# A transformer block on one core: a plain second MLP product, a coarser convolution and coarser modulation sums

## The chip, the cores and the metric

The kernel runs on one core of a Trainium2 chip. The metric is the device time of one execution, in microseconds (us). The core has a matrix engine (PE, whose weight loads the profile shows apart as PEld), a vector engine (DVE), a scalar engine (ACT), a general engine (POOL), and a queue for loads and stores (SP). Every engine works through its own list of instructions in order, and an instruction at the head of a list that waits for another engine holds up everything behind it on that list.

## The reference

One block of depth 1 works on 1024 tokens of width 1024, with 256 context tokens, all in fp32. Cut to what the change touches:

```python
mx = jnp.split((s_c @ w_ada[l] + b_ada[l])[:, None, :], N_ADA, axis=-1)      # six modulation vectors
qkv = jax.nn.silu(depthwise_conv_centred(concat([p[3], p[4], p[5]]), conv_w)) # 7 taps, 3 x 8 heads x 128
q = l2_normalize(hd(q)) * DN_HEAD_DIM ** -0.5
k = l2_normalize(hd(k))                                                       # x * rsqrt(sum(x*x) + eps)
h_x = layer_norm(ALPHA * h_x + mx[2] * y_x, ln1_g[l], ln1_b[l])
h_x = layer_norm(ALPHA * h_x + mx[5] * (jnp.square(jax.nn.relu(u @ w1)) @ w2), ln2_g[l], ln2_b[l])
```

`u @ w1` is 1024 x 1024 by 1024 x 4096, and the second MLP product is 1024 x 4096 by 4096 x 1024. The gated delta rule (DeltaNet) runs for 8 heads in both directions over chunks of 128 tokens. Then come 8 heads of differential attention over the same tokens.

## The kernel before, in words

Every large product is made of three matmuls of rounded parts: an operand is cast to fp32r by ACT (the high part), DVE or POOL subtracts that from the fp32 value (the low part), and hi x hi, hi x lo and lo x hi are added up in one PSUM bank. A matmul has a 128 x 128 left operand and a moving operand of up to 512 columns.

A scheduler inside the tile framework sets each engine's order from priorities and its own estimates of durations. `rank` puts a piece of work into one of several classes: the delta rule's chain and the weights come first (class 0), `dn_prep` and the inverse after them (1), the convolution after that (2).

The stages that the change touches, in order of time:

- **DeltaNet** (`dn_phase`, about 190 to 1330 us). Per head, `dn_proj` multiplies the tokens by a weight block for k, q and v, ACT copies the products into `cvraw`, and a convolution of 7 taps follows: one ACT row for the middle tap and six DVE rows `L441` for the others, for each stretch of `CW` = 256 columns. k and v have five such stretches (one of context, four of tokens), q has four. `dn_prep` builds chunk matrices; `rsqrt` (L126 to L137) takes the reciprocal root of the squared norms by a bit trick and four Newton rounds of three DVE rows (L134 to L136). `inverse32` (L547 to L578) inverts the diagonal blocks in one long chain of dependent DVE rows, `dn_double` completes the inverse on PE, and `dn_chain` walks the ten chunks in both directions (PE, DVE `xs` L674 and `S` L689, ACT). Its end calls `rsqrt` again, scales the head's output (L715), and PE transposes that (L719). POOL subtracts the low parts of the weights (L152).
- **Attention** (`da_all`, about 1330 to 2095 us). While a head's scores run, `ada_cols` adds up the modulation vectors of 4 or 5 column blocks of 128: per block four loads of 128 KB (`adraw`, two buffers, two rows of 128 columns per partition each) and eight DVE rows (L1461, L1463).
- **First MLP product** (`mlp_up`, to 2684 us): a Strassen-Winograd scheme with seven products in place of eight. It stays as it is.
- **Second MLP product** (`mlp_down`, from 2686 us to the end): the same scheme. The 32 row blocks of w2 are taken in six groups, the tokens in four pairs of blocks, and each group and pair has seven products. Per product DVE adds a bank of 512 columns into `acc` (L1421). Before that the sums and differences of the blocks must be made: of `araw` on DVE (L1329), of `braw` on POOL (L1325) after POOL has scaled it (L1365), and all seven forms of each are split (ACT L1320, DVE or POOL L1322). `feed` sets how far ahead the operands are made (`DAA`, `DBA`), and most operand tiles have one buffer. After its last product a token block gets its layer norm on DVE and is stored.

Of the kernel before, what the change touches and what calls it, by code (L numbers as in the profile page):

```python
# [17 lines left out]
P = 128  # L18
# [18 lines left out]
CW = 256  # L37
# [6 lines left out]
DAA, DBA = (14, 14)  # L44
LPB = (2, 3)
S1 = 8
AB = (2, 1, 1, 1, 1, 1, 1)
DG = (2, 2, 3, 3, 3, 3)
# [7 lines left out]
class K:  # L56
# [69 lines left out]
    def rsqrt(self, pool, x, n, tag):  # L126
# [6 lines left out]
        for _ in range(4):  # L133
# [283 lines left out]
    def dn_proj(self, h, nm, res):  # L417
# [6 lines left out]
        raw = self.dw.tile([P, T + 12], F32, name="cvraw", bufs=2)  # L424
        XO = CTX + 9
        nc.gpsimd.memset(raw[:, XO - 3:XO], 0.0)  # L426
        nc.gpsimd.memset(raw[:, XO + SEQ:XO + SEQ + 3], 0.0)
        if not isq:
            nc.gpsimd.memset(raw[:, 0:3], 0.0)
            nc.gpsimd.memset(raw[:, 3 + CTX:6 + CTX], 0.0)  # L430
            nc.gpsimd.dma_start(out=raw[:, 3:3 + CTX], in_=self.kvc_d[0 if nm == "k" else 1, h])
        self.gemm_cols(w, (self.uh, self.ul), TOKS_X, lambda ps, t0, n: nc.scalar.copy(out=raw[:, XO + t0:XO + t0 + n], in_=ps))
        acc = self.dw.tile([P, SEQ if isq else T], F32, name=nm + "T", bufs=BK[" vqk".index(nm)])
# [10 lines left out]
        res[nm] = acc  # L444

# [25 lines left out]
    def dn_prep(self, h, r):  # L471
# [7 lines left out]
        for c0, n in groups:  # L479
            pt = self.pt.tile([P, 4, P], F32, name="pt")  # L480
            for c in range(n):
                nc.tensor.transpose(out=pt[:, c, :], in_=ch(kT, c0 + c), identity=self.ident)
# [29 lines left out]
        for c0, n in ((0, NC0), (NC0, 4), (NC0 + 4, 4)):  # L512
            dec = [self.dn_decay(d, h, c0, n, c0 > 0) for d in range(2)]
            pk = self.pt.tile([P, 4, P], F32, name="pt")
            for c in range(n):
                nc.tensor.matmul(pk[:, c], lhsT=ch(kT, c0 + c), rhs=ch(kT, c0 + c), start=True, stop=True)
# [4 lines left out]
            if c0:  # L521
                pk = self.pt.tile([P, 4, P], F32, name="pt")
                for c in range(n):
                    nc.tensor.matmul(pk[:, c], lhsT=ch(kT, c0 + c), rhs=ch(qT, c0 + c - NC0), start=True, stop=True)
# [107 lines left out]
    def dn_pre(self, h, r):  # L632
# [13 lines left out]
        for c0, n in ((0, 4), (4, 4), (8, 2)):  # L646
            pt = self.pt.tile([P, 4, P], F32, name="pt")
            for c in range(n):
                nc.tensor.transpose(out=pt[:, c, :], in_=ch(kT, c0 + c), identity=self.ident)
# [3 lines left out]
    def dn_chain(self, h, r):  # L653
# [9 lines left out]
        for step in range(NT):  # L663
            for d in range(2):
# [6 lines left out]
                else:  # L671
                    nc.tensor.matmul(pc[:, 0], lhsT=ch(kT, c), rhs=S0, start=True, stop=True)
# [628 lines left out]
    def mlp_down(self):  # L1301
        nc, i = self.nc, self.i
        sizes = DG
        at = [sum(sizes[:g]) for g in range(len(sizes))]
# [343 lines left out]
```

## Time and profile before

| | |
|---|---|
| time, median of 3 runs | 3126.78 us (3111.26 to 3156.79) |
| profiled execution, time | 3127.75 us |
| its span, first to last instruction | 3126.0 us |
| PE busy | 2800.6 us, 90% |
| PE's weight loads busy | 2234.6 us, 71% |
| DVE busy | 2315.2 us, 74% |
| ACT busy | 1412.6 us, 45% |
| POOL busy | 984.9 us, 32% |
| mean granted PE clock | 0.951 of full |

The profile is one execution. Matmuls are pipelined, so that their busy time is longer than the distance from one to the next. A view by stages gives, for each stretch, its start and end, its length, the busy time of PE, PEld, DVE, ACT and POOL with the number of instructions in brackets, the share of full clock that PE was granted, the busy share of the DMA engines and the GB/s they moved. A row of waits names an instruction, what released it, the total in us, how often, and the longest. A timeline row has start, duration, engine, line, operation, output and inputs, and in square brackets the idle time before it and its releaser. A group of instructions has its count, the total busy us and the mean in ns, and the idle time before them.

### The profile page before, as it was taken

The page shows a single profiled execution, that of the slowest core. Times are in us where ns is not written, and L with a number is a line of the kernel's source. Part 1 is how long each engine was busy: PE and PEld are TensorE (multiplying, and loading weights), DVE is VectorE, ACT ScalarE, POOL GpSimd, SP SyncE. Part 2 cuts the span into 40 slices and gives each one's busy share as a digit, 9 for nine tenths or more (in the row PEclk, how much of TensorE's full clock was granted, in tenths as well). Part 3 has the DMA queues.
Part 4 walks back from the last instruction along what each step waited for, and adds up shares of the span by engine and source line. Part 5 has one row for each costly group of instructions (what it writes and reads, how often), then busy time and mean ns, then how long its engine had stood idle before and what let it go on. Part 6 is the DMA issues. An engine that isn't in the chain of part 4 may idle for free.

```text
span 3126.0 us, 46024 instructions
## 1 busy us (share of the span) xinstructions
PE 2800.6 (90%) x15736; PEld 2234.6 (71%) x15736; DVE 2315.2 (74%) x4654; ACT 1412.6 (45%) x3547; POOL 984.9 (32%) x973
## 2 busy tenths in 40 slices
PE   7988889899898989989999998999998999777887
PEld 4876668677686767768777776777776777566666
DVE  4658688886876856368888886646658775799989
ACT  4644335345453443335555555655546223233332
POOL 1245313423434242111111110001006433867770
PEclk9999979989998998999999998999999999898999
DMA  7521211211212122363333333127555443422222
GB/s 259 188 91 40 52 50 42 58 46 44 68 40 56 43 50 64 89 152 91 93 94 81 89 87 94 56 75 221 169 156 182 144 128 111 166 72 81 81 81 93
DMA packets 370043, 303.20 MB, mean 97 GB/s; under 512 B 89300, under 2 KB 321876, under 8 KB 368784
## 3 DMA queue, kind: packets, MB, share of 16 engines
q1 hardware_dynamic: 347920, 252.14, 27.5%
q10 hardware_dynamic: 18304, 37.41, 4.8%
q0 software_dynamic: 3584, 10.71, 0.9%
q8 instruction: 124, 2.03, 0.3%
q14 instruction: 111, 0.91, 0.1%
HBM read 212.08 MB, written 66.06 MB: 89 GB/s over the span
## 4 chain that ended last, share of the span: by engine, by line
PE 36%; DVE 16%; DMA 6%; issue 2%; ACT 2%; POOL 0%; SPq 0%; ACTq 0%; DVEq 0%; POOLq 0%
PE pat L912 4%; PE pg L970 4%; PE pg L972 4%; PE pg L971 4%; DVE A L1322 3%; PE pat L909 2%; PE pg L166 2%; PE pg L167 2%; PE pg L168 2%; PE pa L970 2%; DVE acc L1421 2%; PE pa L972 2%; PE pa L971 2%; PE sx L873 2%; PE sx L874 2%
## 5 line engine op out<-in xcount | busy, mean ns | idle before, releaser
L152 POOL TENSOR_TENSOR wlo<-wraw,whi 128x256 fp32r<-128x256 f32 x312 | 357.3, 1150 | 1224.3 <-ACT whi L151 891.4
L168 PE MATMUL pg<-uh,wlo 128*128 128x512 f32 x1152 | 483.4, 420 | 33.0 <-POOL wlo L152 32.8
L166 PE MATMUL pg<-uh,whi 128*128 128x512 f32 x1152 | 484.8, 421 | 12.6 <-ACT whi L151 6.5
L167 PE MATMUL pg<-ul,whi 128*128 128x512 f32 x1152 | 479.8, 416 | 0.0
L151 ACT CAST whi<-wraw 128x256 fp32r<-128x256 f32 (+1 forms) x568 | 240.9, 430 | 334.9 <-DMA wraw<-in_w_in_dram 98.5
L168 PEld LDWEIGHTS pg<-uh,wlo 128*128 128x128 f32 x1152 | 226.3, 196 | 80.4 <-POOL wlo L152 40.3
L166 PEld LDWEIGHTS pg<-uh,whi 128*128 128x128 f32 x1152 | 225.7, 196 | 53.6 <-ACT whi L151 7.8
L167 PEld LDWEIGHTS pg<-ul,whi 128*128 128x128 f32 x1152 | 225.3, 196 | 39.5
L152 DVE TENSOR_TENSOR wlo<-wraw,whi 128x256 fp32r<-128x256 f32 (+1 forms) x256 | 134.3, 533 | 117.8 <-ACT whi L151 113.6
L884 DVE TENSOR_REDUCE mp<-sx 128x1 f32<-128x1024 f32 x128 | 155.8, 1219 | 40.5 <-PE sx L874 40.1
L970 PE MATMUL pa<-B,A 128*128 128x512 f32 x256 | 109.7, 429 | 79.6 <-DVE acc L1421 45.3
L1320 ACT CAST A<-araw 128x384 fp32r<-128x384 f32 (+1 forms) x144 | 66.2, 476 | 238.7 <-DVE araw L1329 105.3
L889 ACT ACTIVATE p<-sx,mx 128x1024 f32<-128x1024 f32 x128 | 143.2, 1119 | 55.8 <-DVE mx L885 50.8
L912 PEld LDWEIGHTS pat<-V,aT 128*128 128x128 f32 x1280 | 149.2, 192 | 14.9 <-ACT aT L910 12.8
L912 PE MATMUL pat<-V,aT 128*128 128x128 f32 x1280 | 157.3, 278 | 0.0
L441 DVE SCALAR_TENSOR_TENSOR vT<-cvraw,taps,vT 128x256 f32<-128x256 f32 x240 | 120.4, 525 | 13.5 <-ACT vT L439 12.6
L1322 DVE TENSOR_TENSOR A<-araw,A 128x384 fp32r<-128x384 f32 (+1 forms) x144 | 126.6, 886 | 2.7 <-ACT A L1320 2.3
L909 PE MATMUL pat<-ident,p 128*128 128x128 f32 x640 | 119.3, 285 | 6.7 <-ACT aT L910 2.4
L970 PEld LDWEIGHTS pa<-B,A 128*128 128x128 f32 x256 | 51.7, 202 | 101.3 <-ACT A L1320 44.0
L1463 DVE SCALAR_TENSOR_TENSOR adacc<-adraw,s_cols,adacc 128x128 f32<-128x128 f32 x224 | 84.9, 379 | 52.1 <-DMA adraw<-in_w_ada_dram 48.3
L441 DVE SCALAR_TENSOR_TENSOR kT<-cvraw,taps,kT 128x256 f32<-128x256 f32 x240 | 114.9, 509 | 4.8 <-POOL cvraw L426 4.7
L909 PEld LDWEIGHTS pat<-ident,p 128*128 128x128 f32 x640 | 74.7, 142 | 56.7 <-ACT aT L910 22.6
(479 smaller groups left out, 7739.9 us busy)
## 6 DMA issues: line engine op xcount, KB each, us to landing
wraw<-in_w_in_dram SPq DMA_DIRECT2D x288, 128.0 KB
wraw<-in_w_in_dram SPq DMA_DIRECT2D x64, 256.0 KB
adraw<-in_w_ada_dram SPq DMA_DIRECT2D x128, 128.0 KB
uraw<-in_w_mlp_dram SPq DMA_DIRECT2D x32, 512.0 KB
braw<-in_w_mlp_dram SPq DMA_DIRECT2D x32, 512.0 KB
ff_d<-ue SPq DMA_DIRECT2D x52, 256.0 KB
araw<-ff_d SPq DMA_DIRECT2D x32, 384.0 KB
wa<-in_w_ada_dram SPq DMA_DIRECT2D x8, 1024.0 KB
```

The source lines that it names most:

```text
L151: nc.scalar.copy(out=hi, in_=raw)
L152: self.weng.tensor_tensor(out=lo, in0=raw, in1=hi.bitcast(F32), op=ALU.subtract)
L166: nc.tensor.matmul(o, lhsT=hi, rhs=a, start=k == 0, stop=False)
L167: nc.tensor.matmul(o, lhsT=hi, rhs=b, start=False, stop=False)
L168: nc.tensor.matmul(o, lhsT=lo, rhs=a, start=False, stop=k == KT - 1)
L441: nc.vector.scalar_tensor_tensor(out=a, in0=raw[:, t0 - 3 + j:t0 - 3 + j + n], scalar=self.taps[:, j, s:s + 1], in1=a, op0=ALU.mult, op1=A ...
L909: nc.tensor.transpose(out=pt[:, c], in_=a[:, (c0 + c) * P:(c0 + c + 1) * P], identity=self.ident)
L912: nc.tensor.matmul(po, lhsT=aT[:, c], rhs=r["v"][:, c], start=c == 0, stop=c == NT - 1)
L970: nc.tensor.matmul(ps, lhsT=ah, rhs=bh, start=k == 0 and not add, stop=False, **more)
L971: nc.tensor.matmul(ps, lhsT=ah, rhs=bl, start=False, stop=False, **more)
L972: nc.tensor.matmul(ps, lhsT=al, rhs=bh, start=False, stop=k == n - 1, **more)
L1322: eng.tensor_tensor(out=z[1], in0=x, in1=z[0].bitcast(F32), op=ALU.subtract)
```

## The change

- The second MLP product is a plain one: four groups of eight row blocks of w2, eight token blocks, 1024 output columns in two banks. That is 4 x 8 x 8 x 2 x 3 = 1536 matmuls of 512 columns, where 6 groups' seven products made 7 x 4 x 16 x 3 = 1344. Each row block of w2 is scaled (DVE) and split once (ACT cast, DVE subtraction), with 12 buffers for the split blocks, 3 for the raw ones; each token block of `ff` is split once per group, with 3 buffers. POOL does nothing there. `acc` is added to 64 times in place of 168.
- The convolution has two parts per tensor in place of five or four: the context and the tokens stand in one buffer with a gap of 8 columns, cut where the first product of 512 tokens ends. k and v have parts of 772 and 516 columns, q of 508 and 516; six DVE rows each, so 12 in place of 30 or 24. `ck` steps over the gap.
- `rsqrt` has three Newton rounds.
- `ada_cols` loads one row block of w_ada for all of a head's columns at once (320 or 256 KB, 640 or 512 columns per partition) into a single buffer and adds it in one DVE row: 8 loads and 8 rows per head in place of 16 or 20 loads and 32 or 40 rows.

```diff
@@ rsqrt
-        for _ in range(4):
+        for _ in range(3):
@@ dn_proj
-        raw = self.dw.tile([P, T + 12], F32, name="cvraw", bufs=2)
-        XO = CTX + 9
+        raw = self.dw.tile([P, T + GAP + 6], F32, name="cvraw", bufs=2)
+        XO = CTX + GAP + 3
...
-            c0 = 0 if isq else CTX
-            for t0, o, n in ([] if isq else [(3, 0, CTX)]) + [(XO + t, c0 + t, CW) for t in range(0, SEQ, CW)]:
-                a = acc[:, o:o + n]
-                nc.scalar.activation(out=a, in_=raw[:, t0:t0 + n], func=AF.Copy, scale=self.taps[:, 3, s:s + 1])
+            at = XO - 3 if isq else 0
+            cut = SPLIT if isq else CTX + GAP + SPLIT
+            for o, e in ((0, cut), (cut, acc.shape[1])):
+                a = acc[:, o:e]
+                nc.scalar.activation(out=a, in_=raw[:, at + 3 + o:at + 3 + e], func=AF.Copy, scale=self.taps[:, 3, s:s + 1])
                 for j in (0, 1, 2, 4, 5, 6):
-                    nc.vector.scalar_tensor_tensor(out=a, in0=raw[:, t0 - 3 + j:t0 - 3 + j + n],
+                    nc.vector.scalar_tensor_tensor(out=a, in0=raw[:, at + j + o:at + j + e],
                                                    scalar=self.taps[:, j, s:s + 1], in1=a, op0=ALU.mult, op1=ALU.add)
@@ mlp_down (the old body, shown above, is taken out)
+        G, NK = 4, 8
+        shapes = {"acc": ([P, NX, D], F32, 1), "mx5": ([P, D], F32, 1), "lng": ([P, D], F32, 2), "araw": ([P, NK, P], F32, 2),
+                  "braw": ([P, D], F32, 3), "A": ([P, 2, NK, P], F32R, 3), "B0": ([P, 2, D], F32R, 2), "B": ([P, 2, D], F32R, NB2 - 2)}
...
+        def split(z, x):
+            nc.scalar.copy(out=z[:, 0], in_=x)
+            nc.vector.tensor_tensor(out=z[:, 1], in0=x, in1=z[:, 0].bitcast(F32), op=ALU.subtract)
+            return z
...
+        def make_b(n):
+            if n not in raws:
+                load_b(n)
+            r = raws.pop(n)
+            nc.vector.tensor_tensor(out=r, in0=r, in1=mx5, op=ALU.mult)
+            B[n] = split(tile("B0" if n % NB2 < 2 else "B"), r)
...
+        make_a(0, 0)
+        make_b(2)
...
+        for n in range(3, NK):
+            make_b(n)
+        for t in range(NX):
+            nc.scalar.dma_start(out=acc[t], in_=self.ah_d[t * P:(t + 1) * P, :])
+        make_a(0, 1)
+        gb = []
+        steps = [(g, t) for g in range(G) for t in range(NX)]
+        for n, (g, t) in enumerate(steps):
+            if n + 2 < len(steps):
+                load_a(*steps[n + 2])
+            a = A.pop((g, t))
+            ps = [p.tile([P, 512], F32, name=nm) for p, nm in ((self.pa, "pa"), (self.pg, "pg"))]
+            for k in range(NK):
+                bt = B[NK * g + k]
+                for c in range(2):
+                    s = slice(512 * c, 512 * c + 512)
+                    mm = lambda x, y, **kw: nc.tensor.matmul(ps[c], lhsT=a[:, x, k], rhs=bt[:, y, s], **kw)
+                    mm(0, 0, start=k == 0, stop=False)
+                    mm(0, 1, start=False, stop=False)
+                    mm(1, 0, start=False, stop=k == NK - 1)
+                if t == NX - 1 and g + 1 < G and k < NK - (NB2 - NK):
+                    make_b(NK * (g + 1) + NB2 - NK + k)
+            if n + 2 < len(steps):
+                make_a(*steps[n + 2])
+            if g + 1 < G and 2 <= t < 2 + NB2 - NK:
+                make_b(NK * (g + 1) + t - 2)
...
+            for c in range(2):
+                d = acc[t][:, 512 * c:512 * c + 512]
+                nc.vector.tensor_tensor(out=d, in0=ps[c], in1=d, op=ALU.add)
+            if g == G - 1:
+                self.layer_norm(w, acc[t], *gb, acc[t], True)
...
@@ ada_cols
-        for c in range(c0, c0 + n):
-            a = acc[:, c - c0]
-            for k in range(0, KT, 2):
-                raw = self.das.tile([P, 2, P], F32, name="adraw", bufs=2)
...
+        a = acc.rearrange("p n c -> p (n c)")
+        for k in range(KT):
+            raw = self.das.tile([P, n * P], F32, name="adraw", bufs=1)
+            nc.sync.dma_start(out=raw, in_=i["w_ada"][0, k * P:(k + 1) * P, (16 + c0) * P:(16 + c0 + n) * P])
+            sc = self.s_cols[:, k:k + 1]
...
+                nc.vector.scalar_tensor_tensor(out=a, in0=raw, scalar=sc, in1=a, op0=ALU.mult, op1=ALU.add)
```

Three places in DVE's list show what moves. The first is the end of the seventh head in DeltaNet, where the last head's inverse (`slY`, `slX`) runs beside the convolution (`vT`) and the seventh head's second `rsqrt` (`soa`, `soy`). Before:

```order
L134 TENSOR_TENSOR soa<-soy 128x8
L441 SCALAR_TENSOR_TENSOR vT<-cvraw,taps,vT 128x256
L135 SCALAR_TENSOR_TENSOR soa<-soa,so 128x8
L561 TENSOR_TENSOR slY<-slX,slL 104x200
L136 SCALAR_TENSOR_TENSOR soy<-soa,soy 128x8
L441 SCALAR_TENSOR_TENSOR vT<-cvraw,taps,vT 128x256
L714 TENSOR_TENSOR soy<-soy,rq 128x8
L562 TENSOR_REDUCE slX<-slY 104x2x10
L715 TENSOR_TENSOR oacc<-oacc,soy 128x1024
L561 TENSOR_TENSOR slY<-slX,slL 104x242
L441 SCALAR_TENSOR_TENSOR vT<-cvraw,taps,vT 128x256
L562 TENSOR_REDUCE slX<-slY 104x2x11
```

Now, with the lines of the changed kernel (L440 is the convolution, L719 the scaling of the output):

```order
L132 TENSOR_TENSOR soa<-soy 128x8
L565 TENSOR_TENSOR slY<-slX,slL 104x392
L133 SCALAR_TENSOR_TENSOR soa<-soa,so 128x8
L566 TENSOR_REDUCE slX<-slY 104x2x14
L134 SCALAR_TENSOR_TENSOR soy<-soa,soy 128x8
L565 TENSOR_TENSOR slY<-slX,slL 104x450
L718 TENSOR_TENSOR soy<-soy,rq 128x8
L566 TENSOR_REDUCE slX<-slY 104x2x15
L719 TENSOR_TENSOR oacc<-oacc,soy 128x1024
L573 TENSOR_TENSOR slY<-slX,slL 104x1024
L725 SCALAR_TENSOR_TENSOR sz<-po,dng,sz 128x512 x2
L575 TENSOR_REDUCE slL<-slY 104x4x16
```

Both pieces begin at the last Newton round, the fourth before and the third now. Before, convolution rows stand in that round, between it and the scaling of the output (L715), and behind that: the piece has three, and five more follow among the inverse's next rows. Now none stands from the last round's start to the inverse's end; the convolution of `vT` is through before it. Over the whole list, 544 rows belong to the steps that the chain and the completion of the inverse are made of (`z`, `xs`, `S`, `oacc`); before, 64 of them stand right behind a run of convolution rows (247 rows in these runs), now 38 do (76 rows).

The second place is DVE's list in the attention stage, where a head's modulation sums begin: the second head's before, the sixth's now. Before:

```order
L1461 TENSOR_SCALAR adacc<-adraw,s_cols 128x128 [waits DMAHW0_49,PE_49]
L1470 TENSOR_TENSOR mxc<-pg,bc 128x5
L1463 SCALAR_TENSOR_TENSOR adacc<-adraw,s_cols,adacc 128x128 [waits DVE_49]
L1463 SCALAR_TENSOR_TENSOR adacc<-adraw,s_cols,adacc 128x128 [waits DMAHW1_49,DVE_49]
L1463 SCALAR_TENSOR_TENSOR adacc<-adraw,s_cols,adacc 128x128 [waits DVE_49]
L884 TENSOR_REDUCE mp<-sx_14582 128x1 [waits PE_49]
L893 TENSOR_TENSOR sm<-sp 128x2 [waits Activation_49]
L1463 SCALAR_TENSOR_TENSOR adacc<-adraw,s_cols,adacc 128x128 [waits DMAHW2_49,DVE_49]
L895 RECIPROCAL rs<-sm 128x2 [waits DVE_49]
L1463 SCALAR_TENSOR_TENSOR adacc<-adraw,s_cols,adacc 128x128 [waits DVE_49]
```

Now (L1411 and L1413 are the sums; the names in brackets are what a row waits for, `DMAHW` a load from the SP or ACT queue):

```order
L1411 TENSOR_SCALAR adacc<-adraw,s_cols 128x512 [waits DMAHW3_49,PE_49]
L1420 TENSOR_TENSOR mxc<-pg,bc 128x4
L1422 TENSOR_SCALAR mxc<-mxc 128x8 [waits DVE_49]
L1413 SCALAR_TENSOR_TENSOR adacc<-adraw,s_cols,adacc 128x512 [waits DMAHW2_49]
L897 TENSOR_TENSOR sm<-sp 128x2 [waits Activation_49]
L899 RECIPROCAL rs<-sm 128x2 [waits DVE_49]
L901 SCALAR_TENSOR_TENSOR cf<-sm,rs,nlam 128x1 [waits DVE_49]
L903 SCALAR_TENSOR_TENSOR p_17268<-p_17268,cf,p_17265 128x1280 [waits DVE_49,PE_49]
L887 TENSOR_REDUCE mp<-sc 128x2 [waits PE_49]
L1413 SCALAR_TENSOR_TENSOR adacc<-adraw,s_cols,adacc 128x512 [waits DMAHW4_49]
```

Before, a load brings the data of two rows, and a second buffer is loaded meanwhile; now every row needs a load of its own, which can't start before the row ahead of it has read the one buffer. Between the first and the second row of the piece DVE has two small rows, between the second and the third five. On SP's queue the next load stands behind the same wait, ahead of weight loads.

The third is DVE's list in the second MLP product. Before, in the middle of the stage:

```order
L1329 TENSOR_TENSOR araw<-araw 128x3x128
L1421 TENSOR_TENSOR acc<-pa,acc 128x512
L1329 TENSOR_TENSOR araw<-araw 128x3x128
L1329 TENSOR_TENSOR asum<-araw 128x384
L1322 TENSOR_TENSOR A_27414<-araw,A_27414 128x384
L1322 TENSOR_TENSOR A_27295<-araw,A_27295 128x384
L1322 TENSOR_TENSOR A_27352<-araw,A_27352 128x384
L1322 TENSOR_TENSOR A_27379<-asum,A_27379 128x384
L1322 TENSOR_TENSOR B_27417<-braw,B_27417 128x512
L1421 TENSOR_TENSOR acc<-pg,acc 128x512
L1322 TENSOR_TENSOR A_27435<-araw,A_27435 128x384
```

Now, at the end of the first group (L1386 adds a bank to `acc`, L1319 subtracts, L1332 scales):

```order
L1386 TENSOR_TENSOR acc<-pa,acc 128x512
L1386 TENSOR_TENSOR acc<-pg,acc 128x512
L1319 TENSOR_TENSOR A<-araw,A 128x1024
L1319 TENSOR_TENSOR B_26126<-braw,B_26126 128x1024
L1319 TENSOR_TENSOR B_26138<-braw,B_26138 128x1024
L1319 TENSOR_TENSOR B<-braw,B 128x1024
L1332 TENSOR_TENSOR braw<-braw,mx_25615 128x1024 x2
L1319 TENSOR_TENSOR B<-braw,B 128x1024
L1386 TENSOR_TENSOR acc<-pa,acc 128x512
L1386 TENSOR_TENSOR acc<-pg,acc 128x512
L1319 TENSOR_TENSOR A<-araw,A 128x1024
```

Per token block two additions and one subtraction are left, and the four row blocks of the next group that must wait for a free buffer come in one burst.

## Rows read from the trace of the kernel before


**Rows 1.** The page: its head.

```profile
span 3126.0 us, 46024 instructions
```

**Rows 2.** Stages: start, end, us, busy (instructions) per engine, clock, DMA share, GB/s.

```profile
190.00:1330.00 1140.00, 1018.42 (x6789) 818.31 (x6787) 840.75 (x2162) 504.57 (x1440) 405.10 (x456) 0.93 0.20 52
1330.00:2095.00 765.00, 718.42 (x4143) 578.95 (x4141) 580.43 (x1127) 429.37 (x1111) 93.15 (x108) 0.98 0.34 88
2400.00:2686.00 286.00, 270.49 (x1146) 212.91 (x1144) 190.50 (x238) 76.08 (x144) 126.89 (x97) 0.99 0.46 136
2686.00:3126.00 440.00, 341.34 (x1344) 266.51 (x1344) 406.04 (x519) 136.01 (x287) 274.22 (x185) 0.90 0.28 92
```

**Rows 3.** PE's waits in the last stage (us, times, longest).

```profile
PE pa L970 <- DVE acc L1421: 45.3, 18, 5.1
PE pa L970 <- ACT A L1320: 31.9, 4, 8.9
```

**Rows 4.** PE's timeline, first MLP product: first and last of 57 matmuls.

```profile
2659.60 0.39 PE L970 MATMUL pa<-za,uo 128*128 128x512 f32 x1
...
2672.29 0.39 PE L972 MATMUL pa<-za 128*128 128x512 f32 x1
```

**Rows 5.** Timeline of PE: first and last matmul of the last stage.

```profile
2686.36 0.49 PE L970 MATMUL pa<-B,A 128*128 128x512 f32 x1 [2.21 <-ACT B L1320]
...
3116.16 0.40 PE L972 MATMUL pa<-B,A 128*128 128x512 f32 x1
```

**Rows 6.** Last stage's groups by line and shape (busy us, mean ns).

```profile
L1322 DVE TENSOR_TENSOR B<-braw,B 128x512 fp32r<-128x512 f32 x23 | 29.3, 1274 | 0.0
L1421 DVE TENSOR_TENSOR acc<-pa,acc 128x512 f32<-128x512 f32 x96 | 64.8, 681 | 9.1 <-PE pa L972 9.1
L1060 DVE SCALAR_TENSOR_TENSOR acc<-acc,lnmv,braw 128x1024 f32<-128x1024 f32 x8 | 10.2, 1280 | 0.1
L1320 ACT CAST B<-braw 128x512 fp32r<-128x512 f32 x64 | 36.2, 616 | 11.2 <-PE pa L972 8.1 <-issue 1.7 <-PE pg L972 1.2
```

**Rows 7.** Timeline, DVE and POOL: a subtraction alone, one beside POOL.

```profile
2690.09 0.68 DVE L1322 TENSOR_TENSOR B<-braw,B 128x512 fp32r<-128x512 f32 x1
...
2705.24 1.44 POOL L1325 TENSOR_TENSOR bsum<-braw,bsum 128x512 f32<-128x512 f32 x1
2705.48 1.74 DVE L1322 TENSOR_TENSOR B<-bsum,B 128x512 fp32r<-128x512 f32 x1
```

**Rows 8.** Busy time in 20 us of the last stage (columns: Rows 2).

```profile
2706.00:2726.00 20.00, 13.66 (x47) 10.28 (x48) 19.26 (x23) 3.14 (x8) 19.84 (x15) 0.73 0.73 259
```

**Rows 9.** Busy time, sum over DeltaNet's 520-580, 660-700, 780-840, 900-960, 1040-1100 us.

```profile
sum 280.00, PE 245.94 PEld 193.36 DVE 277.29 ACT 127.24 POOL 122.77; mean PE 49.19 PEld 38.67 DVE 55.46 ACT 25.45 POOL 24.55
```

**Rows 10.** Lines L441 and L1463: ns min/median/max, first and last start.

```profile
L441 DVE SCALAR_TENSOR_TENSOR kT<-cvraw,taps,kT x240: 467/478/1852, 186.8 to 1099.5; 128x256 f32<-128x256 f32 x120
L1463 DVE SCALAR_TENSOR_TENSOR adacc<-adraw,s_cols,adacc x224: 330/352/928, 1316.0 to 1879.7; 128x128 f32<-128x128 f32 x112
```

**Rows 11.** DVE's timeline: a Newton round's first row, and the next's.

```profile
1308.69 0.17 DVE L134 TENSOR_TENSOR soa<-soy 128x8 f32<-128x8 f32 x1
...
1309.29 0.17 DVE L134 TENSOR_TENSOR soa<-soy 128x8 f32<-128x8 f32 x1
```

**Rows 12.** PE's waits in the DeltaNet stage, 190 to 1330 us.

```profile
PE pg L168 <- POOL wlo L152: 32.8, 13, 9.8
PE po L719 <- DVE oacc L715: 24.9, 8, 6.2
```

**Rows 13.** DVE's waits in the attention stage, 1330 to 2095 us.

```profile
DVE adacc L1463 <- DMA adraw<-in_w_ada_dram: 42.0, 26, 6.6
DVE adacc L1461 <- DMA adraw<-in_w_ada_dram: 15.3, 11, 2.5
```

**Rows 14.** Timeline, SP's queue and DVE: an adraw load, its first reader.

```profile
1350.46 0.86 SPq L1456 DMA_DIRECT2D adraw<-in_w_ada_dram  x1
...
1356.57 0.81 DVE L1463 SCALAR_TENSOR_TENSOR adacc<-adraw,s_cols,adacc 128x128 f32<-128x128 f32 x1 [6.64 <-DMA adraw<-in_w_ada_dram]
```

More of the change, by code (lines that the diff above doesn't have):

```diff
@@ L36 @@
 ORD = 'vkqffz'
-CW = 256
+GAP = 8
+SPLIT = 508
 W1 = (2, 4)
@@ L515, in dn_prep @@
             for c in range(n):
-                nc.tensor.matmul(pk[:, c], lhsT=ch(kT, c0 + c), rhs=ch(kT, c0 + c), start=True, stop=True)
+                nc.tensor.matmul(pk[:, c], lhsT=self.ck(kT, c0 + c), rhs=self.ck(kT, c0 + c), start=True, stop=True)
             for c in range(n):
@@ L671, in dn_chain @@
                 else:
-                    nc.tensor.matmul(pc[:, 0], lhsT=ch(kT, c), rhs=S0, start=True, stop=True)
+                    nc.tensor.matmul(pc[:, 0], lhsT=self.ck(kT, c), rhs=S0, start=True, stop=True)
                     xs = ds.tile([P, P], F32, name=f"xs{d}", bufs=1)
@@ L1315, in mlp_down @@
         nc.scalar.dma_start(out=mx5, in_=self.mx5_d.to_broadcast((P, D)))
-        araw, braw, bank, gb = {}, {}, {}, []
-        turn = iter(range(10000))
-        def split(z, x, share):
-            nc.scalar.copy(out=z[0], in_=x)
-            eng = nc.gpsimd if share == (1, 1) or share[0] and next(turn) % share[1] < share[0] else nc.vector
-            eng.tensor_tensor(out=z[1], in0=x, in1=z[0].bitcast(F32), op=ALU.subtract)
-        def tt(o, x, y, op):
-            nc.gpsimd.tensor_tensor(out=o, in0=x, in1=y, op=op)
-            return o
@@ L1374, in make_b @@
-        def make_b(key):
-            g, p = key
-            z = tile(f"B{p}")
-            for k in range(sizes[g]):
-                while (g, k) not in braw or p > 4 and pending and pending[0][0] == (g, k):
-                    step()
-                split((z[:, 0, k], z[:, 1, k]), braw[g, k][p], LPB if g else (int(k > 0), 1))
-            if g == LAST and p == 4:
-                for n in ("ln2_g", "ln2_b"):
-                    x = tile("braw")
-                    nc.scalar.dma_start(out=x, in_=i[n].to_broadcast((P, D)))
-                    gb.append(x)
-            return z
@@ L1388, in mlp_down, with load_b @@
-        pending = [((0, k), load_b(0, k)) for k in range(sizes[0])]
-        def step():
-            if pending and next(pending[0][1], 1):
-                pending.pop(0)
-                step()
-        while len(pending) >= sizes[0]:
-            step()
+        def split(z, x):
+            nc.scalar.copy(out=z[:, 0], in_=x)
+            nc.vector.tensor_tensor(out=z[:, 1], in0=x, in1=z[:, 0].bitcast(F32), op=ALU.subtract)
+            return z
+        raws, B, A = {}, {}, {}
+        def load_b(n):
+            raws[n] = tile("braw")
+            nc.sync.dma_start(out=raws[n], in_=i["w_mlp2"][0, n * P:(n + 1) * P])
@@ new lines, in mlp_down @@
+        make_a(0, 1)
[20 more added lines that the diff above has]
+                make_b(NK * (g + 1) + t - 2)
+            if g == G - 1 and t == 0:
+                for nm in ("ln2_g", "ln2_b"):
+                    gb.append(tile("lng"))
+                    nc.scalar.dma_start(out=gb[-1], in_=i[nm].to_broadcast((P, D)))
+            for c in range(2):
[3 more added lines that the diff above has]
+                self.layer_norm(w, acc[t], *gb, acc[t], True)
+                for c in range(2):
+                    s = slice(512 * c, 512 * c + 512)
+                    (nc.scalar if c else nc.sync).dma_start(out=self.out[0, t * P:(t + 1) * P, s], in_=acc[t][:, s])
```

126 lines of the change are left out of this document (23 added, 103 removed).

## The prediction

> **What bounds the kernel now.** I read the stages first, since the shares of the whole span mix different limits. In the DeltaNet stage (1140 us) PE is busy for 1018 us and DVE for 841; in the attention stage (765 us) PE for 718; in the last stage, the second MLP product (440 us), PE for only 341, DVE for 406 [rows 2]. The last stage is the one that PE doesn't bound: the reader is to see DVE at 92% and a granted PE clock of 0.90 there. PE's waits name the cause: 45.3 us for an addition into `acc`, 31.9 us for the split of an operand [rows 3]. DVE is slow there because POOL works beside it: a subtraction of 512 columns takes 0.68 us alone and 1.74 us while a POOL row runs [rows 7], 1.27 us in the mean [rows 6]. The first MLP product shows what PE can do: 57 matmuls start within 12.69 us, 0.2266 us apart [rows 4]; with its stalls that stage needs 286 us for 1146, or 0.2496 us each, at a clock of 0.99 [rows 2].
>
> In DeltaNet the mean hides two regimes. In five stretches of 280 us together DVE is busy for 277 us, and PE for 246 [rows 9]: there the chain of inverse, convolution and small rows on DVE sets the pace, and PE is short of work for 34 us.
>
> **The second MLP product.** Before, it runs from PE's first matmul at 2686.36 us to the end of the span at 3126.0 us [rows 1, 5]. After, PE has 1536 matmuls in place of 1344: 1536 x 0.2266 = 348.1 us. DVE has 32 row blocks x 2 passes and 32 token splits of 1024 columns, 96 x 1.28 us (the row of 1024 columns [rows 6], with POOL idle) = 123 us, 64 additions x 0.681 = 44 us [rows 6], and eight layer norms of two such long rows and some 1.6 us of statistics, 33 us: 200 us in all. ACT has 64 casts of 1024, at most 2 x 0.616 us each [rows 6] = 79 us. PE is the bound by far, so POOL's 274 us [rows 2] and DVE's sums vanish without a new wait, except in two places.
>
> At the start the first token block needs eight row blocks of w2, of which two or three are ready; the others cost DVE 2 x 1.28 = 2.56 us each while PE uses one in 6 x 0.2266 = 1.36 us. Five or six times the difference is about 7 us. The loads of `acc` (8 x 512 KB), `braw` and `araw` fall into the same 20 us; the queues moved 259 GB/s at most there [rows 8], and some 7 MB would need 27 us, of which I charge 5. So 12 us. At the group ends four row blocks come in one burst, 4 x 2.56 us of DVE in a token block's 48 x 0.2266 = 10.9 us, with 15 us until the first is used: nothing. The tail, from the last matmul's start to the end, stays at 3126.0 - 3116.16 = 9.8 us [rows 1, 5].
>
> Low end: 2686.4 + 348.1 + 9.8 = 3044.3, or -82 us. High end, with the first MLP product's pace, 1536 x 0.2496 = 383 us, and the 12 us: 3091.6, or -34. I take a clock of 0.98 (between that stage's 0.99 and the attention stage's [rows 2]), 355 us, and the 12 us: 3063, or **-63 us**.
>
> **The convolution.** Before, 672 rows of 478 ns [rows 10] are 321 us of DVE. The same operation takes 352 ns for 128 columns [rows 10] and 1280 ns for 1024 [rows 6]: 1.036 ns a column and 219 ns a row. The new rows are thus 1.02 us (772 columns), 0.75 us (516) and 0.75 us (508): per head 12 x 1.77 + 6 x 1.50 = 30.3 us, 242 us in all, 79 us less. It is the fixed 219 ns of 384 rows that goes.
>
> **The Newton rounds.** A round is three rows, 0.60 us [rows 11]. Sixteen calls in DeltaNet give 9.7 us, eight of them on the way to the transposes for which PE waits 24.9 us [rows 12]. The calls in attention and the norm I cost at nothing: other DVE and PE work lies around them.
>
> Of these 89 us of DVE, what reaches the end is what PE can take. PE's idle time in the five stretches is 34 us; the first and last heads and POOL's weight splits, on which PE waits 32.8 us [rows 12] and which DVE delays as in [rows 7], add some. I take half, **-45 us**. Bounds: -89, and 0 if the chain waits elsewhere. A loss I exclude, though a row is now up to 1.02 us long: fewer of the chain's rows stand behind convolution rows than before (38 for 64, behind 76 rows for 247).
>
> **The modulation sums.** 224 x 0.352 us and 32 first rows become 32 rows of 0.88 us and 24 of 0.75: about 42 us less DVE. But DVE isn't what binds attention: PE is at 94% with a clock of 0.98 [rows 2]. Against it stands the single buffer. Today DVE waits 57.3 us for `adraw` [rows 13], and one load shows 6.1 us from its issue to its first reader, though it moves only 128 KB, since the queues were full [rows 14]. After, 56 loads of 256 or 320 KB each wait for the row before. Between 0 and 56 x 6.1 = 342 us of DVE waiting is possible; the order puts other rows between most pairs, so I take about today's 57 us, and with the 42 us as a reserve **0** (-20 to +40).
>
> The Trainium skill, "DMA: Bandwidth & Descriptors", section "Anatomy of one DMA", gives a fixed 2 us per transfer plus its bytes at 436 GB/s, measured on the GpSimd path; as an estimate that is 2.75 us for 320 KB, 154 us for all if each were exposed, and the sum would come to 3117 us in place of mine. This trace's load is slower than the page's.
>
> **Sum.** The profiled execution took 3127.75 us, 1 us above the median of the runs. 3127.75 - 63 - 45 = **3020 us**.
>
> **Rivals.**
> 1. The forecast, MLP gain and half of DeltaNet's: 2985 to 3045, chance 0.55.
> 2. DeltaNet gives nothing: its PE is busy for 89% of the stage and a shorter DVE list only makes DVE wait. For it: in the stage's mean PE is fuller than DVE. Against: [rows 9]. 3127.75 - 63 = 3065 (3045 to 3085); 0.22.
> 3. DVE's relief arrives in full, and the clock rises: 3127.75 - 82 - 89 - 20 = 2937 (to 2985); 0.13.
> 4. The plain product doesn't run at PE's pace: the three raw buffers or the start leave PE stalls, and the 14% more matmuls eat half of the gain. At the high end above, with DeltaNet's 0: 3094 (3085 to 3150); 0.06. For it: PE waited for operands on four occasions of up to 8.9 us [rows 3].
> 5. Slower: the single `adraw` buffer. In attention DVE also makes the maxima that the scores wait for, and a sum that waits for its load holds them up. If all 56 loads are exposed at 6.1 us, 3020 + 342 - 57 = 3305. It decides from (108 + 57) / 56 = 2.9 us per load on: above that the whole change is slower than before. Against: DVE has 185 us of slack there, and most pairs have other rows between them. 0.04.
>
> The Trainium skill, "Trainium Kernel Development and Optimization", section "Best Practices", asks for two buffers so that loads and compute overlap, which speaks for this rival; no row of the kernel before has one buffer.
>
> A measurement of this kernel tells about 2% (63 us) from no change, so "faster" ends at 3064 us. Rivals 1 and 3 are faster, and half of 2; rival 4 and the other half of 2 lie within 2%: faster 0.80, same 0.17, slower 0.03. The range 2955 to 3082 holds rival 1, most of 2 and half of 3, about 0.8.
>
> **What would show it.** In the changed profile the last stage should have PE at 0.227 us a matmul, a clock near 1, no POOL, DVE around half busy, and end some 375 us after its first matmul; waits on `acc` should be gone, and waits on B appear only in the first 20 us. In DeltaNet the 18 convolution rows per head should take 30 us, DVE's full stretches be shorter, and the stage end about 45 us earlier; if it ends as late as before with more DVE idle time, rival 2 holds. In attention the wait on `adraw` should stay near 57 us; at 150 us or more, with the stage longer, rival 5 is at work. The forecast is wrong if the MLP stage needs more than 405 us, or DeltaNet's end moves by less than 10 or more than 90 us.

## The result, and the profile after

The changed kernel takes 3039.72 us (median of 4 runs, 3028.13 to 3048.91) against 3133.51 us for the kernel before, which ran beside it again (4 runs in all). The ratio is 0.970, 95% interval 0.962 to 0.978. The forecast was 3020 us, its range 2955 to 3082.

The head of the page of the changed kernel and its PE line:

```profile
span 3036.9 us, 44469 instructions
...
PE 2828.2 (93%) x15928; PEld 2273.6 (75%) x15928; DVE 2008.3 (66%) x3675; ACT 1333.1 (44%) x3269; POOL 656.6 (22%) x756
```

By stages, each cut at the same event as in [rows 2] (columns as there): DeltaNet, attention, the first and the second MLP product.

```profile
190.00:1311.00 1121.00, 1025.84 (x6775) 826.79 (x6774) 798.94 (x1725) 492.12 (x1379) 369.78 (x440) 0.92 0.20 53
1311.00:2066.00 755.00, 722.05 (x4149) 583.92 (x4149) 539.35 (x910) 431.01 (x1112) 92.60 (x109) 0.98 0.35 90
...
2375.00:2660.50 285.50, 268.46 (x1144) 211.90 (x1144) 194.48 (x244) 77.46 (x143) 107.09 (x80) 1.00 0.47 138
2660.50:3036.90 376.40, 355.72 (x1536) 291.74 (x1536) 179.76 (x201) 66.04 (x70) 0.00 (x0) 0.97 0.32 106
```

The four lines answer to those of [rows 2] one by one. The last stage went from 440 us to 376.4, DeltaNet from 1140 to 1121, attention from 765 to 755, and the first MLP product stayed. The reader is to see in the last line that POOL is at 0.00, DVE at 180 us in place of 406, and the granted clock at 0.97 in place of 0.90; in the first line that DVE lost 42 us, but PE's busy time *rose* by 7 us for nearly the same number of matmuls (6775 for 6789 in the stretch), at a clock of 0.92 in place of 0.93.

What PE still waits for in the second MLP product (us, times, longest), beside [rows 3]:

```profile
PE pa L1370 <- ACT B L1318: 5.0, 1, 5.0
PE pa L1370 <- DVE B L1319: 3.4, 2, 2.5
PE pa L1370 <- DVE A L1319: 2.9, 2, 2.4
PE pa L1370 <- ACT A L1318: 2.3, 1, 2.3
```

All of these six waits lie in the first 30 us. The waits on `acc`, 45.3 us before, are gone. DVE's groups there (busy us, mean ns, then idle time before):

```profile
L1319 DVE TENSOR_TENSOR A<-araw,A 128x1024 fp32r<-128x1024 f32 x32 | 38.9, 1220 | 12.2 <-ACT A L1318 12.2
L1319 DVE TENSOR_TENSOR B<-braw,B 128x1024 fp32r<-128x1024 f32 x30 | 36.1, 1221 | 4.7 <-ACT B L1318 3.5
L1386 DVE TENSOR_TENSOR acc<-pa,acc 128x512 f32<-128x512 f32 x32 | 22.1, 690 | 157.0 <-PE pa L1370 157.0
```

The split of 1024 columns takes 1220 ns with POOL idle, where one of 512 took 1274 beside POOL [rows 6]; and it is DVE that waits for PE now, 157 us.

PE's waits in DeltaNet, beside [rows 12]:

```profile
PE po L723 <- DVE oacc L719: 25.8, 7, 11.0
PE pg L166 <- POOL wlo L150: 5.8, 5, 1.8
```

The wait for the scaled output is the same, 25.8 us for 24.9; the wait for POOL's weight splits fell from 32.8 us to 5.8. DVE's wait for a modulation load in attention, beside [rows 13] (57.3 us in two lines):

```profile
DVE adacc L1413 <- DMA adraw<-in_w_ada_dram: 37.1, 21, 5.4
```

### The profile page after: what moved, and what is told of

Its sections match the earlier page's. It is cut to its first block, busy times and chain, and to the rows that moved or that the text cites. A ratio compares the mean times of both kernels' runs of the same rounds, so it can differ in the third digit from the quotient of the medians.

```text
span 3036.9 us, 44469 instructions
## 1 busy us (share of the span) xinstructions
PE 2828.2 (93%) x15928; PEld 2273.6 (75%) x15928; DVE 2008.3 (66%) x3675; ACT 1333.1 (44%) x3269; POOL 656.6 (22%) x756
## 5 line engine op out<-in xcount | busy, mean ns | idle before, releaser
L150 POOL TENSOR_TENSOR wlo<-wraw,whi 128x256 fp32r<-128x256 f32 x312 | 320.7, 1033 | 1219.5 <-ACT whi L149 987.3
L1370 PE MATMUL pa<-B,A 128*128 128x512 f32 x768 | 220.6, 395 | 13.6 <-ACT B L1318 5.0
L1370 PE MATMUL pg<-B,A 128*128 128x512 f32 x768 | 219.5, 393 | 0.0
L1370 PEld LDWEIGHTS pa<-B,A 128*128 128x128 f32 x768 | 145.9, 190 | 46.9 <-ACT B L1318 5.4
L1370 PEld LDWEIGHTS pg<-B,A 128*128 128x128 f32 x768 | 146.2, 190 | 30.7
L1386 DVE TENSOR_TENSOR acc<-pa,acc 128x512 f32<-128x512 f32 x32 | 22.1, 690 | 157.0 <-PE pa L1370 157.0
L1318 ACT CAST A<-araw 128x1024 fp32r<-128x1024 f32 x32 | 33.6, 1052 | 209.7 <-PE pg L1370 171.8
L877 PE MATMUL sx<-K,Q 128*128 128x512 f32 x256 | 109.5, 428 | 2.9 <-DMA wraw<-in_w_in_dram 2.0
```

Source lines behind the costliest of these rows:

```text
L150: self.weng.tensor_tensor(out=lo, in0=raw, in1=hi.bitcast(F32), op=ALU.subtract)
L1370: mm = lambda x, y, **kw: nc.tensor.matmul(ps[c], lhsT=a[:, x, k], rhs=bt[:, y, s], **kw)
```

## The experiments

Every ratio below is to the kernel before, run on the same chip beside the kernel in question, with its 95% interval.

**The four parts alone.** Each kernel is the one before with one of the four bullets of the change and nothing else. The plain product:

```diff
@@ mlp_down (the whole new body)
-        sizes = DG
+        G, NK = 4, 8
```

> The kernel before with the plain second MLP product alone. Theory: the stage's 63 us in the comparison of the two traces are all its own, the ratio to before is 0.980 (about 3070 us), the stage takes 376 us, DeltaNet and attention stay where they were. Rival: the 19 us of DeltaNet and the 10 us of attention are scatter between two executions and the product carries the whole change, ratio 0.971 (about 3043 us).

Measured: 0.980 (0.975 to 0.985), 3063 us. In its profile the last stage takes 374.6 us and DeltaNet ends at 1314.0 us (the start of its last transpose; 1314.5 before). The theory held; the product's 64 us are its own.

The convolution:

```diff
@@ dn_proj
+            for o, e in ((0, cut), (cut, acc.shape[1])):
```

> The kernel before with the two-part convolution alone. Theory: DVE's time falls by about 46 us in DeltaNet (0.40 us of DVE's time for a row of 256 columns, 0.67 for 516 and 0.94 for 772, not the durations of 0.48, 0.75 and 1.02), and some 40% of it reach the end: DeltaNet ends 15 to 22 us earlier, ratio 0.993 to 0.995. Rival 1: all that DVE saves arrives, 45 us, ratio 0.985. Rival 2: DeltaNet is PE's and nothing arrives, ratio 1.000.

Measured: 0.990 (0.9875 to 0.9925), 31 us, with DeltaNet's end at 1283.0 us. More than the theory's 22 and less than rival 1's 45; neither reading of DVE's time hit it.

The modulation sums:

```diff
@@ ada_cols
+            raw = self.das.tile([P, n * P], F32, name="adraw", bufs=1)
```

> The kernel before with the whole-head modulation sums alone. Theory: DVE's relief of about 40 us in attention lets PE wait less for the softmax, -5 to -10 us, ratio 0.997 to 0.998. Rival 1: no effect, ratio 1.000, the 10 us of the comparison were scatter. Rival 2: the single load buffer holds the softmax up, +10 us or more, ratio 1.003 or above, with the waits on adraw over 60 us.

Measured: 0.9998 (0.9976 to 1.002), and DVE's wait on `adraw` in the later sums is 49.6 us for 42.0 before. Rival 1: the sums do nothing, in either direction.

Three Newton rounds:

```diff
-        for _ in range(4):
+        for _ in range(3):
```

> The kernel before with three Newton rounds alone. Theory: 48 rows fewer in DeltaNet, 8 to 10 us of DVE, at most 5 us at the end, ratio 0.998 to 1.000. Rival: the round lies on the way to the eight waits of PE for the scaled output, the waits fall from 25 us to 20 and the time by 10 us, ratio 0.997.

Measured: 0.992 (0.989 to 0.996), 24 us, beyond both. And the four ratios multiply to 0.962, while the whole change has 0.970, with 0.962 at the very end of its interval: the parts of DeltaNet seem not to add.

**Is it the Newton round's own time?** The scheduler lays out every engine's list anew when a row falls away. Compared row by row in the traces, PE's list up to the end of DeltaNet is the same with the plain product alone as before; only about a half of it stands in the same sequence with three rounds, and about a quarter with the new convolution. So two kernels in which the round's time and the order point different ways:

```diff
@@ rsqrt, in the changed kernel
-        for _ in range(3):
+        for _ in range(4):
```

> The changed kernel with the fourth Newton round put back. Three rounds alone brought 0.992. Theory (order): that gain is not the 48 rows' own time but the order that the scheduler then lays out, and with the new convolution it is laid out anew anyway; the kernel has the DeltaNet order of the convolution alone, so its ratio to before is the product of the single parts, 0.9796 x 0.990 x 0.9998 = 0.9696 (3034 us), no slower than the whole change at 0.9698. Rival (own time): a round is on PE's way and costs 24 us here too, ratio 0.977 to 0.978 (about 3058 us).

Measured: 0.969 (0.966 to 0.973). With the fourth round the change is as fast as with three, and the product of the single parts, 0.980 x 0.990 = 0.970, holds: no time of the round's own shows there. (The whole change's own interval is wider, 0.962 to 0.978, so that this pair alone is weak evidence.)

```diff
@@ rsqrt, in the kernel before
-        for _ in range(4):
+        for _ in range(5):
```

> The kernel before with five Newton rounds: the suspected cost doubled in the other direction. Theory (own time): as the fourth round costs 24 us, so does a fifth, ratio 1.007 to 1.008. Rival (order): the rows' own 10 us of DVE bring at most 5 us, and the order scatters by 20 us to either side: anything from 0.993 to 1.008, with no reason to lie on the slower side; a ratio of 1.000 or less excludes the own time.

Measured: 0.9975 (0.995 to 1.000). A fifth round makes the kernel no slower, which excludes 24 us as its own time. And two rounds in the changed kernel:

```diff
@@ rsqrt, in the changed kernel
-        for _ in range(3):
+        for _ in range(2):
```

> The changed kernel with two Newton rounds; the third round of the reciprocal roots is left out. Theory (order): DVE's 10 us bring at most 5, and the new order up to 20 us to either side, ratio to before 0.963 to 0.976. Rival (own time): another 24 us, ratio 0.962 (about 3010 us).

Measured: 0.967 (0.962 to 0.972), which fits the theory and doesn't exclude the rival's 0.962.

**Is it DVE's time?** Another size of the old stretches first:

```diff
-CW = 256
+CW = 512
```

> The kernel before with convolution stretches of 512 columns in place of 256: 384 rows in place of 672, where the change has 288. By DVE's time per row (0.40 us for 256 columns, 0.67 for 512) DVE saves 288 x 0.13 = 37 us in DeltaNet, against 46 for the two parts. Theory (DVE's relief): the end follows in proportion, 0.8 of the two parts' 31 us, 25 us, ratio 0.992. Rival (order): no proportion, between 1.000 and 0.985.

Measured: 0.999 (0.996 to 1.003). DVE's busy time in the stage fell by 26 us (835 to 809), and nothing came. The same stretches in the changed kernel, in place of the two parts:

```diff
@@ dn_proj, in the changed kernel: the old body, and
+CW = 512
```

> The changed kernel with the convolution of before, in stretches of 512 columns. Alone such stretches brought nothing (0.999) though DVE saves 37 us. Theory 1 (they never bring anything, the two parts do by something that the stretches lack): 0.9796, the plain product alone. Theory 2 (that kernel's order was a bad one of a scatter of 20 us): 0.970 to 0.973, as with the two parts.

Measured: 0.967 (0.963 to 0.971), just beyond theory 2 and as with the two parts. It doesn't show that the stretches bring something here that they don't bring alone. Theory 1 forgot the three rounds, which this kernel has too: the single ratios of the product, the sums, the rounds and the stretches (0.980, 0.9998, 0.992, 0.999) multiply to 0.971. What it shows is that in the change the stretches do as well as the two parts, although alone the two parts were 0.9% faster.

Then DVE's time put back without its being needed:

```diff
@@ dn_proj, in the changed kernel, behind the six taps
+                for j in ((2, 4, 5) if o else ()):
+                    nc.vector.scalar_tensor_tensor(out=a, in0=raw[:, at + j + o:at + j + e],
+                                                   scalar=0.0, in1=a, op0=ALU.mult, op1=ALU.add)
```

> The changed kernel with three more DVE rows for the second part of every tensor's convolution, with a factor of zero, so that nothing is added: 72 rows of 0.67 us, 48 us of DVE, which is what the new convolution saves. Theory (DVE's time): the gain of the two parts goes again, ratio to before 0.978 to 0.980. Rival (DVE's time is hidden, the gain comes from something else in the two parts or from the order): the ratio stays at 0.970, between 0.966 and 0.974.

Measured: 0.972 (0.968 to 0.976). Its DeltaNet, from 190 us to its last transpose, and the changed kernel's:

```profile
190.00:1292.90 1102.90, 1003.21 (x6763) 807.92 (x6762) 834.14 (x1791) 498.10 (x1383) 374.04 (x444) 0.93 0.20 51
```

```profile
190.00:1295.50 1105.50, 1012.26 (x6718) 816.11 (x6717) 795.52 (x1718) 488.14 (x1371) 368.07 (x437) 0.92 0.19 50
```

DVE is busy for 834 us again, as before the change (835), for 39 us more than in the changed kernel, and the stage takes no more time than there. (This execution was the fastest of its six; the ratio, of all six, says the same.) The rival held: the time that the convolution frees on DVE is nearly all hidden time. And DVE's time taken away, by leaving out three of the six taps that DVE adds:

```diff
-                for j in (0, 1, 2, 4, 5, 6):
+                for j in (1, 2, 4):
```

> The changed kernel with three of the six DVE taps of the convolution left out: 144 rows fewer, half of 231 us, 115 us of DVE less in DeltaNet. Theory (DVE's time): as 46 us brought 31, 115 us bring some 70, ratio to before 0.945 to 0.950. Rival (hidden): DeltaNet is PE's by now, whose matmuls and clock don't change, and at most 15 us come, ratio 0.965 or above.

Measured: 0.962 (0.958 to 0.966), 25 us less than the whole change: between the two, nearer to the rival.

```profile
190.00:1258.80 1068.80, 995.05 (x6685) 803.59 (x6684) 688.28 (x1574) 476.33 (x1360) 343.09 (x434) 0.93 0.20 51
```

107 us less DVE than in the changed kernel, and less than a quarter of that at the end. The last two kernels ran on the same chip and can be set against each other: 146 us of DVE's time (834 to 688) are worth 31 us at the end (3043 to 3012 us), a fifth.

**What made the old second product slow?** The kernel before, without POOL's scaling and its sums:

```diff
@@ load_b
-                for c in (0, 512):
-                    nc.gpsimd.tensor_tensor(out=r[j][:, c:c + 512], in0=r[j][:, c:c + 512], in1=mx5[:, c:c + 512], op=ALU.mult)
...
-            for o, x, y in ((t1, b12, b11), (t2, b22, t1), (b12, b22, b12), (t4, b21, t2)):
-                tt(o, x, y, ALU.subtract)
+            for _ in range(4):
```

> The kernel before, whose second MLP product leaves out POOL's scaling of w2's row blocks and POOL's sums and differences of them; the splits (DVE and POOL), DVE's sums of the token blocks and its 168 additions into acc stay. PE's 1344 matmuls need 305 us at full clock; the stage took 440, with 98 us of idle PE and 39 lost to the clock. Theory (POOL's work beside DVE is what makes DVE too slow): DVE's rows come near their 0.68 us, PE's idle time falls to 45 us or less and the clock follows, stage 360 to 375 us, ratio to before 0.975 to 0.980, as with the plain product. Rival (DVE's own list and the single-buffered operands set the pace): the stage falls by 20 us or less, ratio 0.993 or above.

Measured: 0.981 (0.978 to 0.985). The last stage, PE's two longest waits in it, and the split of 384 columns on DVE, there and in the kernel before:

```profile
2678.50:3052.50 374.00, 322.71 (x1344) 258.13 (x1344) 327.50 (x517) 136.48 (x286) 109.48 (x73) 0.95 0.32 107
```

```profile
PE pa L970 <- DVE acc L1417: 27.1, 13, 4.2
PE pa L970 <- ACT A L1320: 7.2, 1, 7.2
```

```profile
L1322 DVE TENSOR_TENSOR A<-araw,A 128x384 fp32r<-128x384 f32 x96 | 68.2, 713 | 0.7 <-ACT A L1320 0.5
```

```profile
L1322 DVE TENSOR_TENSOR A<-araw,A 128x384 fp32r<-128x384 f32 x96 | 89.6, 936 | 0.5 <-ACT A L1320 0.3
```

The theory held in the main: the ratio is just above its 0.980, the stage takes 374 us, and PE's idle time is 51 us where it said 45 or less. The split went from a mean of 936 ns to 713, though DVE's list is as long as before (517 rows for 519 in the stage) and PE's is the same row for row; DVE's busy time went from 406 us to 328, the waits on `acc` from 45.3 to 27.1 and those on the cast of A from 31.9 to 7.2 [rows 3]. The rows also show how: in the kernel before, counted over all rows of L1322 of that size, the 45 that no POOL row overlapped took 0.55 us in the median, the 67 others 1.05; here 76 have no POOL row beside them, and take 0.55 too. That POOL's own results came late is not the cause: PE waited for a POOL row for 3.7 us in the whole stage before, DVE for none. So POOL's rows beside DVE's made the stage slow. And seven products without POOL's scaling and sums, with all the rest that they need, are no faster than the plain product with 14% more matmuls.

## Why the prediction was right

The total is 20 us above the forecast and inside its range; the sign and the size hold because the largest term did. The second term, DeltaNet's, has the right sign, but by luck more than by its reason: most of what came there isn't the DVE time that the forecast charged it to.

**The second MLP product** (forecast -63): -64 us in the ratio, -63.4 between the two traces. Its inner parts can be read off too. PE's idle time in the stage fell from 98.7 us to 20.7, which is -78. PE's busy time rose by 14, although 192 matmuls at 0.2266 us are 43.5: by that estimate the other 29 came back through the clock, 0.97 for 0.90. The forecast took 0.98 and 12 us at the start; 0.97 and 13.6 us of waits were measured. DVE's sum of 200 us was 180.

**The modulation sums** (forecast 0): 0.9998 alone. The single buffer did not hold the softmax up, and 42 us less DVE brought nothing where PE is busy for 94%. The Trainium skill, "Trainium Kernel Development and Optimization", section "Best Practices", asks for two buffers; here one was as good, most likely because the engine that waits for it has time to wait.

**DeltaNet** (forecast -45): 0.990 in the ratio of the whole change to the plain product, 31 us, and 19 us between the two traces. With both intervals that ratio is good to 0.01 only, but the two parts alone gave the same 0.990 to within 0.0025. The traces alone can't settle such a figure: three kernels whose PE and DVE lists are row for row the same up to the second MLP product (before, the plain product alone, the old product without POOL's sums) took 1124.5, 1124.0 and 1107.3 us for it; two with the same lists up to its end (the two parts alone, the change with four rounds) took 1093.0 and 1105.8. Two steps of the term were wrong.

First, the saving on DVE was mis-sized: 79 us forecast, about 50 by the starts. I took a row's time to be its recorded duration, 0.48 us for 256 columns. In the trace of before, a convolution row and the row behind it:

```profile
558.00 0.47 DVE L441 SCALAR_TENSOR_TENSOR vT<-cvraw,taps,vT 128x256 f32<-128x256 f32 x1
558.39 0.86 DVE L561 TENSOR_TENSOR slY<-slX,slL 104x392 f32<-104x392 f32 x1
```

The next row starts 0.39 us after the first, while that one still shows 0.08 us of its 0.47. After, for 516 and for 772 columns:

```profile
549.98 0.75 DVE L440 SCALAR_TENSOR_TENSOR qT<-cvraw,taps,qT 128x516 f32<-128x516 f32 x1
550.65 0.68 DVE L575 TENSOR_REDUCE slL<-slY 104x64 f32<-104x512 f32 x1
...
598.10 1.02 DVE L440 SCALAR_TENSOR_TENSOR vT<-cvraw,taps,vT 128x772 f32<-128x772 f32 x1
599.03 0.34 DVE L678 SCALAR_TENSOR_TENSOR xs<-pc,necg,vtok 128x128 f32<-128x128 f32 x1
```

0.67 and 0.93 us, where the durations are 0.75 and 1.02. The durations that I had forecast, 0.75 and 1.02, came true (the shorter ones in ns as min/median/max over all heads):

```profile
L440 DVE SCALAR_TENSOR_TENSOR qT<-cvraw,taps,qT x96: 725/743/1527, 198.3 to 1089.4; 128x508 f32<-128x508 f32 x48, 128x516 f32<-128x516 f32 x48
```

but the 79 us were a difference of durations. By the starts it is 672 x 0.40 less 96 x 0.94, 144 x 0.67 and 48 x 0.66, about 50 us for undisturbed rows; the stage's busy time, which counts overlapping rows once, fell by 42 with the Newton rows in it, and by 40 (835 to 795) with the two parts alone. The Trainium skill has this in "Perfetto Trace Analysis", section "Optimizing Scalar/DVE Operations": the second half of a row's fixed latency, in which its write is acknowledged, overlaps with the next row. The trace agrees, with 0.08 to 0.09 us per row. The overlap is there where the next row doesn't depend on the first: in a Newton round, where it does, a row of 0.17 us takes 0.20 from start to start [rows 11].

Second, "I take half" of what DVE saves. The runs with DVE's time put back (+39 us, +0.2% of the time, within the interval of none) and with half the taps left out (-107 us, 0.8% or 25 us of the time) price it at a quarter or less, the two set against each other at a fifth. Of the 50 us some 10 arrive, not the half. On this point rival 2 was nearer to the truth than the forecast.

What can be said of the rest of the 31 us is in the table. All windows go from 190 us to the start of DeltaNet's last transpose; idle is the window less PE's busy time.

| kernel | DVE busy, us | PE idle, us | clock | PE's wait for POOL's splits, us | ratio | without the plain product's 0.980 |
|---|---|---|---|---|---|---|
| before | 835 | 120 | 0.93 | 32.8 | 1 | 1 |
| the plain product alone | 832 | 110 | 0.92 | 27.7 | 0.980 | 1 |
| the old product without POOL's sums | 840 | 105 | 0.94 | 24.2 | 0.981 | - |
| five rounds | 848 | 114 | 0.93 | 26.5 | 0.9975 | 0.9975 |
| three rounds | 832 | 107 | 0.94 | 27.4 | 0.992 | 0.992 |
| stretches of 512 | 809 | 107 | 0.94 | 24.7 | 0.999 | 0.999 |
| two parts | 795 | 105 | 0.94 | 3.8 | 0.990 | 0.990 |
| the change, four rounds | 796 | 104 | 0.93 | 4.8 | 0.969 | 0.989 |
| the change | 796 | 93 | 0.92 | 5.8 | 0.970 | 0.990 |
| the change, two rounds | 787 | 93 | 0.93 | 12.4 | 0.967 | 0.987 |
| the change, zero rows | 834 | 100 | 0.93 | 8.2 | 0.972 | 0.992 |
| the change, stretches of 512 | 803 | 100 | 0.94 | 16.6 | 0.967 | 0.987 |
| the change, three taps | 688 | 74 | 0.93 | 3.3 | 0.962 | 0.982 |

The columns up to the waits are of one execution each, the ratios of all runs; the execution with stretches of 512 in the kernel before was the fastest of its ten, 3098 us where their median is 3122. The ratio doesn't follow DVE's busy time. What falls with the two parts in every surrounding is PE's wait for POOL's weight splits: 24 to 33 us with stretches of 256 in the kernel before, 3 to 8 us with two parts and three or four rounds (12.4 with two). The trace shows how DVE makes such a wait. POOL's split of 256 columns in the kernel before, once while DVE has convolution rows one after another, and once just after:

```profile
696.99 5.88 POOL L152 TENSOR_TENSOR wlo<-wraw,whi 128x256 fp32r<-128x256 f32 x1 [3.54 <-ACT whi L151]
...
702.90 0.73 POOL L152 TENSOR_TENSOR wlo<-wraw,whi 128x256 fp32r<-128x256 f32 x1
...
693.50 5.23 DVE L441 SCALAR_TENSOR_TENSOR kT<-cvraw,taps,kT 128x256 f32<-128x256 f32 x13
698.65 0.48 DVE L441 SCALAR_TENSOR_TENSOR qT<-cvraw,taps,qT 128x256 f32<-128x256 f32 x1
699.04 0.48 DVE L441 SCALAR_TENSOR_TENSOR kT<-cvraw,taps,kT 128x256 f32<-128x256 f32 x1
699.44 2.86 DVE L441 SCALAR_TENSOR_TENSOR qT<-cvraw,taps,qT 128x256 f32<-128x256 f32 x7
```

(Where a row has x7, seven rows of its kind stand one behind another, with their times in one.) The split starts at 696.99 us, amid 22 convolution rows that run on DVE without a gap from 693.50 to 702.30, and ends at 702.87, just behind them; the next one takes 0.73 us. All splits of DeltaNet up to 1300 us (ns min/median/max), before, with two parts, and with stretches of 512:

```profile
L152 POOL TENSOR_TENSOR wlo<-wraw,whi x188: 712/771/12054, 193.9 to 1291.3; 128x256 fp32r<-128x256 f32 x188
```

```profile
L155 POOL TENSOR_TENSOR wlo<-wraw,whi x194: 718/740/5016, 194.4 to 1296.8; 128x256 fp32r<-128x256 f32 x194
```

```profile
L152 POOL TENSOR_TENSOR wlo<-wraw,whi x192: 715/746/12385, 196.3 to 1292.9; 128x256 fp32r<-128x256 f32 x192
```

The median is nearly the same; the longest is 12.05, 5.02 and 12.39 us. (With two parts and two rounds it is 10.55: an order can bring the long runs back.) My prediction named POOL's splits as a part of the gain, but charged them to DVE's load; the load isn't what decides, since the zero rows leave the wait at 8.2 us. Nor is it shown that these waits carry the 31 us, and the table speaks against most of it. The ratio doesn't follow them: the change with stretches of 512 has 16.6 us of them and stands at 0.987, the change itself 5.8 us and 0.990, three rounds alone 27.4 us and 0.992. PE's whole idle time hardly does either: the three kernels with the old lists have 105 to 120 us of it, with 24 to 33 us of these waits; the two with the lists of two parts and four rounds have 105 and 104, with 4 and 5. So where the waits for POOL went, other waits mostly came. What brings the rest of the 31 us, some 20, stays open. The order that the scheduler lays out is the suspect, since it changes with every one of these edits and three rounds brought 24 us alone and nothing in the change; but no run changed the order and kept every row.

The pair of traces shows less than the ratios, 19 us: PE's idle time fell by 26 us (121.6 to 95.2 in [rows 2] and its counterpart), and its busy time rose by 7 us at the lower clock. That part is scatter as far as is known: over DeltaNet the granted clock was 0.93, 0.92 and 0.94 in the three kernels with the same lists.

**The rivals.** Rival 1, the forecast, came true within its 2985 to 3045. Rival 3's 89 us in DeltaNet and rival 4's stalls in the last stage did not come. Rival 5 needed 2.9 us of waiting per load; 37.1 us over 56 loads are 0.7.

## What to carry to other kernels

Price a row on DVE by the distance between starts, not by its duration, when the next row doesn't depend on it. Where a stage has PE busy for nine tenths, a shorter list on DVE is worth what a run with useless rows put back says, not what its busy time says; and a part's gain measured alone needn't hold beside other parts when a scheduler lays out the order anew. One pair of traces can't price a small change: the same lists gave stages 17 us apart here. Trading fewer matmuls for sums on POOL and DVE didn't pay here, because those sums slowed each other.

## What the runs showed of the hardware

POOL's rows don't only slow down beside DVE: a split of 256 columns, 0.77 us by its median in the kernel before, took up to 12.05 us, and the one shown ended only when 22 convolution rows in a row on DVE had ended. It is no single case: six splits of DeltaNet took over 5 us, each stood beside 14 to 27 DVE rows that followed one another without a gap, nearly all of the convolution, and each ended about 0.6 us behind the last of them. The Trainium skill, "SBUF — State Buffer", section "SBUF: two separate sides", tells of an exclusive lock that an instruction holds for its whole length, so that the other engine is fully blocked; the trace agrees that POOL stands still, and shows the block to outlast any single row of 0.48 us.

In the last stage the granted clock went with PE's idle time, not with its work: 1536 matmuls with 21 us of idle time ran at 0.97, 1344 with 99 us at 0.90, and the same 1344 without POOL's scaling and sums, with 51 us, at 0.95. In DeltaNet it didn't: there 120 us of idle time went with 0.93 and 93 us with 0.92. The stretches below full speed were at 1.2 GHz, half of it; the gain in the last stage is 78 us of idle time and, by the estimate above, 29 us of clock, paid for with 43.5 us of matmuls.
